# Reordering the first loads of a hybrid decoder layer: norm weights, the second column half of x, and who makes the first operand parts

## The chip, the cores and the metric

The kernel runs on one core of a Trainium2 chip. The metric is the device time of one execution in microseconds (us); less is better. The core has TensorE (PE in the profile, PEld for its weight loads), VectorE (DVE), ScalarE (ACT), GpSimd (POOL) and SyncE (SP), and 16 DMA engines, to which transfers are issued from the queues of SyncE (SP) and ScalarE (ACT) here.

## The reference

One layer, 512 tokens of width 1024, in float32: a SwiGLU block, a token mixer, and a second SwiGLU block, each between two RMS norms, with a residual sum. Only the first block's beginning matters here.

```python
def rms_norm(x, g):
    xf = x.astype(jnp.float32)
    y = xf * lax.rsqrt(jnp.mean(xf * xf, axis=-1, keepdims=True) + RMS_EPS)
    return (y * g.astype(jnp.float32)).astype(x.dtype)

def swiglu(x, w_gu, w_down):
    gate, up = jnp.split(x @ w_gu, 2, axis=-1)
    return (jax.nn.silu(gate) * up) @ w_down

def reference(x, ...):
    for l in range(DEPTH):
        x = x + 0.5 * rms_norm(swiglu(rms_norm(x, ffn1_pre_g[l]), ffn1_w_gu[l], ffn1_w_down[l]), ffn1_post_g[l])
        y = hybrid_mixer(rms_norm(x, mix_pre_g[l]), ...)
        x = x + rms_norm(y, mix_post_g[l])
        x = x + 0.5 * rms_norm(swiglu(rms_norm(x, ffn2_pre_g[l]), ffn2_w_gu[l], ffn2_w_down[l]), ffn2_post_g[l])
    return x
```

`ffn1_w_gu` is 1024 x 5632: its columns 0 to 2815 are the gate weights and those from F = 2816 on the up weights.

## The kernel before

**Products in parts.** A float32 product is made from rounded parts. A value v is split into a high part (v rounded to the matmul's type fp32r) and a low part (v minus the high part). A product of w and x is then three matmuls: high w by high x, low w by high x, high w by low x. For weights the high part is a cast on ScalarE (`first_hi`, L1252) and the low part a subtraction on VectorE or another engine (`first_lo`, L1256). For x the two parts are made from the transposed tile in PSUM, with the norm's weight g1 multiplied in: `turned_high` (L641 on ScalarE, L1233 on VectorE) and `turned_low` (L644 on VectorE). The norm's 1/rms is a factor for each token and comes in after the products.

**Tiles.** x lies in HBM by tokens: 512 tokens are four row blocks (b = 0 to 3) of 128, and each is loaded in two column halves (hf = 0, 1) of 512 columns, so `xn[b][hf]` is 128 x 512, 256 KB. TensorE transposes 128 x 128 squares of it, so that columns of x (c = 0 to 7, 128 each, the sum's index) come to lie on partitions. Columns c = 0 to 3 come from hf = 0 and c = 4 to 7 from hf = 1. Tokens are handled in two halves h of 256: h = 0 needs the row blocks 0 and 1, h = 1 the blocks 2 and 3. One PSUM bank `tps[c]` takes the transposes of two columns c and c + 1 for one h.

**The first weights.** The first 128 gate columns and the first 128 up columns are not loaded by the planner of the later weights, but by `load_first(o, i, *queues)`: o = 0 is gate, o = F is up, and i is which half of the 1024 rows (k = 0 to 3, `lower`; k = 4 to 7, `upper`). One such piece is 128 x 512 in SBUF, 256 KB, in rows of 512 bytes in HBM; where two queues are given, each takes half of it. In the code below, `piece(j, i)`, `first_hi(j, i)` and `first_lo(j, i)` have j = 0 for gate and j = 1 for up.

**The order of the head.** Each engine runs its instructions in the order in which the code writes them. Loads (L449 to L461), by queue: SyncE has x(0,0), half of the gate piece 0, the norm weights g1 (8 rows of 128, 4 KB), x(0,1), x(1,1), the gate piece 1, the up-piece 1, then x(2,0), x(3,0), x(2,1), x(3,1) and the planner's first loads. ScalarE has x(1,0), the other half of the gate piece 0, and the whole up-piece 0. TensorE (L1279 on) has seven warm matmuls on a tile of ones (`spin`, each two records in the profile), the eight transposes of h = 0, c = 0 to 3 (`turn_early`, L1214) with the transpose of g1 (L1216) between the second and the third pair, two more warm matmuls, and then the products of the gate piece 0 with c = 0 to 3 (`passes`, L1289): high by high, low by high. Then come the eight transposes of c = 4 to 7 (`turn`, L1224), which need x(0,1) and x(1,1), then the products with the low parts of x; then the up-piece 0 in three passes, then the pieces 1 (`upper`) of both; then the transposes of h = 1 and the same products for it; and from then on the first matmuls of the next weights, `second`.

**Around it.** ScalarE casts gate piece 0, makes the high parts of c = 0 to 3, casts up-piece 0 and gate piece 1, makes the high parts of c = 4 and 5, and casts up-piece 1. VectorE copies g1 out of PSUM (L1282), subtracts for gate piece 0, makes the low parts of c = 0 to 3, subtracts for up-piece 0 and gate piece 1, makes the high parts of c = 6 and 7, and the low parts of c = 4 to 7. GpSimd subtracts for up-piece 1. From about 22 us on the kernel is one long row of matmuls, whose weights a planner (`Weights`) loads, casts and splits some units ahead.

The load part of the head, with its order:

```python
    load_x(0, 0)
    load_x(1, 0, act)
    load_first(0, 0, act, sync)
    load_first(F, 0, act)
    sync.dma_start(g1rows, rows_of("ffn1_pre_g"))
    for b in range(2):
        load_x(b, 1)
    for o in (0, F):
        load_first(o, 1, sync)
```

Of the kernel before, what the change touches and what calls it, by code (L numbers as in the profile page):

```python
# [20 lines left out]
F = 2816  # L21
# [101 lines left out]
def tile_layer(ctx: ExitStack, tc: tile.TileContext, out: bass.AP, **ins: bass.AP):  # L123
    nc = tc.nc
    pe, dve, act, pool, sync = nc.tensor, nc.vector, nc.scalar, nc.gpsimd, nc.sync
# [16 lines left out]
    def bank(name):  # L142
        return psum.tile([P, T], F32, tag="bank", name=name)

    def t2k(name, dt=F32):
        return big.tile([P, T], dt, tag="t2k", name=name, bufs=NT2K)
# [283 lines left out]
    def rows_of(name):  # L430
        a = ins[name]
        return a[0].rearrange("w (c p) -> (w c) p", p=P) if name == "conv_w" else a[0].rearrange("(c p) -> c p", p=P)
# [3 lines left out]
    g1rows = rows_t[:KD, P:2 * P]  # L436
    first_raw = {}

    def load_x(b, hf, queue=sync):
        queue.dma_start(xn[b][hf], ins["x"][0, b * P:(b + 1) * P, hf * T:(hf + 1) * T])  # L440

    def load_first(o, i, *queues):
        r = first_raw[o, i] = t2k(f"first{o}{i}").rearrange("p (k c) -> p k c", k=4)
        n = 4 // len(queues)
        for j, queue in enumerate(queues):
            r0 = i * T + j * n * P
            queue.dma_start(r[:, j * n:(j + 1) * n], w1[0, r0:r0 + n * P, o:o + P].rearrange("(k p) c -> p k c", p=P))

    load_x(0, 0)  # L449
    load_x(1, 0, act)  # L450
    load_first(0, 0, act, sync)
    load_first(F, 0, act)
    sync.dma_start(g1rows, rows_of("ffn1_pre_g"))
    for b in range(2):
        load_x(b, 1)
    for o in (0, F):
        load_first(o, 1, sync)
    for hf in range(2):
# [67 lines left out]
    def product(w, xs, sl=ALL, name="", hooks=()):  # L526
        ps = bank(name)
        hooks = dict(hooks)
        for k, x in enumerate(xs):
            if k in hooks:  # L530
                hooks[k]()
            mm3(ps[:, sl], w, k, [t[:, sl] for t in x], k == 0, k == len(xs) - 1)
        return ps
# [106 lines left out]
    def x_high(x, src, gain, sl):  # L640
        act.activation(x[0][:, sl], src, AF.Copy, scale=gain)  # L641
# [566 lines left out]
    def turn_early():  # L1208

        tp = [bank(f"xtp{c}0") for c in (0, 2)]  # L1210
        for cc in range(4):
            for i in range(2):
                j = cc % 2
                pe.transpose(tp[cc // 2][:, (2 * j + i) * P:(2 * j + i + 1) * P], xn[i][0][:, cc * P:(cc + 1) * P], ident)  # L1214
            if cc == 1:
                pe.transpose(g1_ps[:, :KD], g1rows, ident[:KD, :KD])  # L1216
        return dict(zip((0, 2), tp))

    def turn(h, c):
        tp = bank(f"xtp{c}{h}")  # L1220
        for j in range(2):
            for i in range(2):
                cc = c + j
                pe.transpose(tp[:, (2 * j + i) * P:(2 * j + i + 1) * P], xn[2 * h + i][cc // 4][:, (cc % 4) * P:(cc % 4 + 1) * P], ident)  # L1224
        return tp

    def turned_high(h, c, tp, eng=act):
        for j in range(2):
            x, g = n1.xs[c + j], g1[:, c + j:c + j + 1]
            if eng is act:  # L1230
                x_high(x, tp[:, HALF[j]], g, HALF[h])
            else:
                dve.tensor_scalar(x[0][:, HALF[h]], tp[:, HALF[j]], g, None, op0=ALU.mult)  # L1233
# [12 lines left out]
    def piece(j, i):  # L1246
        (hi, lo), sl = ws[j], slice(4 * i, 4 * i + 4)
        return hi[:, sl, :], lo[:, sl, :], first_raw[(0, F)[j], i]

    def first_hi(j, i):  # L1250
        hi, lo, raw = piece(j, i)
        act.copy(hi, raw)  # L1252

    def first_lo(j, i, eng=dve):
        hi, lo, raw = piece(j, i)
        eng.tensor_sub(lo, raw, hi.bitcast(F32))  # L1256
# [18 lines left out]
    def spin(n):  # L1275
        for i in range(n):
            pe.matmul(warm[:, (i % 4) * P:(i % 4 + 1) * P], ones.bitcast(F32), ones.bitcast(F32), start=True, stop=True)

    spin(WARM)  # L1279
    g1_ps = bank("g1_ps")  # L1280
    tps = turn_early()
    dve.tensor_copy(g1, g1_ps[:, :KD])  # L1282
    spin(2)
    banks = [bank(f"a_first{i}") for i in range(4)]

    def passes(js, ks, part=0, xpart=0, stop=False, sl=HALF[0]):
# [11 lines left out]

    preload(AF.Copy)
    first_hi(0, 0)  # L1300
    turned_high(0, 0, tps[0])
    turned_high(0, 2, tps[2])
    first_lo(0, 0)
    turned_low(0, 0, tps[0])
# [6 lines left out]
    first_hi(1, 0)  # L1311
    first_hi(0, 1)
    turned_high(0, 4, tps[4])
    first_lo(1, 0)
    first_lo(0, 1)
    turned_high(0, 6, tps[6], dve)
    first_hi(1, 1)
# [11 lines left out]
    tps = {c: turn(1, c) for c in range(0, KD, 2)}  # L1329
# [171 lines left out]
    for g, (f0, f1) in enumerate(GROUPS1):  # L1501
# [20 lines left out]
        for c in range(KD):  # L1522
# [18 lines left out]
            b = pair_banks[c] if c < 2 else product(W.take(), xs, name=f"ya{g}{c}")  # L1541
# [6 lines left out]
    def in_product(name, hooks=(), ahead=AHEAD):  # L1548
        return product(W.take(ahead), mx.xs, name=name, hooks=hooks)
# [81 lines left out]
    for j in range(4):  # L1631
        b = in_product(f"pq{j}")
# [254 lines left out]
    tps = [bank(f"atp{ci}") for ci in range(KC)]  # L1887
# [290 lines left out]
```

## Time and profile before

| what | value |
|---|---|
| device time, median of 3 runs | 835.63 us (835.62 to 835.71) |
| the profiled execution, its own time | 836.39 us |
| its span from first to last instruction | 834.6 us |
| matmul records in the span | 4190 |
| bytes moved by DMA | 144.22 MB, 173 GB/s in the mean |

The page gives the busy time of each engine and its share of the span, then groups of instructions. A row of the timeline is: start in us, length in us, engine, line, operation, written tile and read tiles, shape, count, and in brackets the engine's idle time before it with what ended that. Rows that follow one another are merged, so that a length with x4 covers four. The same row with SPq or ACTq shows the issue of a transfer, not the transfer. A row of the waits is: waiting engine and tile, what it waited for, us in total, times, longest. A row of the windows is: the stretch, its length, for PE, PEld, DVE, ACT and POOL the busy time and (count), then TensorE's granted clock, the busy share of the DMA engines, and GB/s.

### The profile page before, as it was taken

To read this page: it belongs to the slowest core of one execution; us is meant where nothing else is said; L and a number is where in the kernel's file an instruction comes from. 1 tells how busy PE (TensorE), PEld (TensorE's weight loads), DVE (VectorE), ACT (ScalarE), POOL (GpSimd) and SP (SyncE) were. 2 spreads that over 40 slices of the span, in tenths; PEclk is the share of its full clock that TensorE was granted. 3 is DMA by queue.
4 is the path that set the end of the run, shared out by engine and by line. 5 is a ranking of instruction groups with operands and counts; after the bars stand their busy time and mean duration, and the time that the engine had idled before them with its cause. 6 is when DMAs were issued, how large, how long until landed. Compare 5 with 4: busy or idle time off the path is not lost.

```text
span 834.6 us, 11761 instructions
## 1 busy us (share of the span) xinstructions
PE 826.2 (99%) x4190; PEld 701.0 (84%) x4190; DVE 733.8 (88%) x1031; ACT 520.0 (62%) x813; POOL 165.5 (20%) x187
## 2 busy tenths in 40 slices
PE   9999999999999999999999999999999999999996
PEld 8888888888888898987788899888888888888885
DVE  5989799998989978888789689998999798898996
ACT  6756756676666654556897446545757677676562
POOL 1022000140320325414531052002005023032001
PEclk9999999999999999999999999999999999999999
DMA  7376408398595797523511140567339949669742
GB/s 254 103 252 244 159 12 308 89 266 259 127 260 180 186 281 230 188 78 94 164 45 51 51 138 15 124 179 253 128 107 240 308 96 250 233 161 261 298 139 102
DMA packets 121835, 144.22 MB, mean 173 GB/s; under 512 B 24168, under 2 KB 76720, under 8 KB 121264
## 3 DMA queue, kind: packets, MB, share of 16 engines
q1 hardware_dynamic: 106896, 112.26, 42.0%
q0 software_dynamic: 13792, 30.42, 16.6%
q10 hardware_dynamic: 1088, 0.79, 0.3%
q8 instruction: 33, 0.54, 0.3%
q14 instruction: 26, 0.21, 0.1%
HBM read 100.45 MB, written 39.32 MB: 167 GB/s over the span
## 4 chain that ended last, share of the span: by engine, by line
PE 98%; DMA 1%; DVE 0%; SPq 0%; issue 0%; DVEq 0%
PE ab L1026 10%; PE aa L1026 10%; PE db L1026 5%; PE da L1026 5%; PE yaa L1427 3%; PE bb L1026 3%; PE ya L1427 3%; PE ba L1026 3%; PE a_first L1289 3%; PE yda L1427 2%; PE aa L956 1%; PE yab L2016 1%; PE yab L2017 1%; PE yab L2018 1%; PE wo L1942 1%; PE gt L522 1%
## 5 line engine op out<-in xcount | busy, mean ns | idle before, releaser
L1198 POOL DMA_DIRECT2D yr_a<-stage x36 | 31.2, 1015 | 175.7 <-ACT stage L1195 153.8
L1198 POOL DMA_DIRECT2D yp_b<-stage x42 | 36.5, 1070 | 146.3 <-ACT stage L1195 120.0
L2032 POOL DMA_DIRECT2D yp_b<-stage x8 | 4.4, 547 | 64.7 <-ACT stage L2031 64.3
L745 POOL TENSOR_TENSOR acca_r<-acca_r,sq_r 128x512 f32<-128x512 f32 x6 | 9.1, 1509 | 38.2 <-ACT sq_r L552 38.1
L540 PE MATMUL an<-xh_mx,whi_xl 128*128 128x256 f32 x64 | 15.7, 285 | 0.0
L541 PE MATMUL an<-xh_mx,wlo_xl 128*128 128x256 f32 x64 | 15.5, 283 | 0.0
L2136 POOL TENSOR_TENSOR last<-yp,grow 128x512 f32<-128x512 f32 x3 | 3.9, 1291 | 57.0 <-DVE yp L2126 57.0
L2133 ACT ACTIVATE ysq<-yp 128x512 f32<-128x512 f32 (+1 forms) x8 | 4.9, 607 | 15.7 <-DVE yp L2126 15.7
L522 PE MATMUL gt<-xh_mx,whi_gt 128*128 128x512 f32 x32 | 14.2, 443 | 0.0
L1464 POOL DMA_DIRECT2D yp_a<-zy x16 | 8.7, 554 | 25.5 <-DMA rows_a<-yr_a 17.2
L498 ACT ACT_TABLE_LOAD x9 | 11.5, 1283 | 2.4 <-issue 2.3
L522 PE MATMUL pq<-xh_mx,whi_q 128*128 128x512 f32 x32 | 12.8, 400 | 0.0
L524 PE MATMUL gt<-xh_mx,wlo_gt 128*128 128x512 f32 x32 | 12.6, 394 | 0.0
L522 PE MATMUL pgb<-xh_f,whi_bg 128*128 128x512 f32 x32 | 12.6, 393 | 0.0
L523 PE MATMUL gt<-xl_mx,whi_gt 128*128 128x512 f32 x32 | 12.5, 392 | 0.0
L524 PE MATMUL pq<-xh_mx,wlo_q 128*128 128x512 f32 x32 | 12.5, 391 | 0.0
L523 PE MATMUL pq<-xl_mx,whi_q 128*128 128x512 f32 x32 | 12.5, 390 | 0.0
L524 PE MATMUL pgb<-xh_f,wlo_bg 128*128 128x512 f32 x32 | 12.5, 390 | 0.0
L524 PE MATMUL pub<-xh_f,wlo_bu 128*128 128x512 f32 x32 | 12.5, 390 | 0.0
L523 PE MATMUL pub<-xl_f,whi_bu 128*128 128x512 f32 x32 | 12.5, 390 | 0.0
L522 PE MATMUL pub<-xh_f,whi_bu 128*128 128x512 f32 x32 | 12.5, 389 | 0.0
L523 PE MATMUL pgb<-xl_f,whi_bg 128*128 128x512 f32 x32 | 12.5, 389 | 0.0
(2028 smaller groups left out, 3397.8 us busy)
## 6 DMA issues: line engine op xcount, KB each, us to landing
yp_b<-stage POOLq DMA_DIRECT2D x50, 256.0 KB, 9.0
yr_a<-stage POOLq DMA_DIRECT2D x44, 256.0 KB, 9.8
h_a<-za SPq DMA_DIRECT2D x16, 256.0 KB
h_b<-zb SPq DMA_DIRECT2D x16, 256.0 KB
hxb<-h_b SPq DMA_DIRECT2D x16, 256.0 KB
hxa<-h_a SPq DMA_DIRECT2D x6, 512.0 KB
raw_ad<-in_ffn_w_down SPq DMA_DIRECT2D x2, 1024.0 KB
xT_hbm<-xT POOLq DMA_DIRECT2D x2, 1024.0 KB, 6.1
```

Of the source, the lines that this page charges most:

```text
L498: act.activation(dummy, eps, func)
L522: pe.matmul(ps, hi[:, k, :], xh, start=start, stop=False)
L523: pe.matmul(ps, hi[:, k, :], xl, start=False, stop=False)
L524: pe.matmul(ps, lo[:, k, :], xh, start=False, stop=stop)
L540: pe.matmul(ps[:, sl], hi[:, k, :], xh, start=k == 0 and not goes_on, stop=False, skip_group_check=True)
L541: pe.matmul(ps[:, sl], lo[:, k, :], xh, start=False, stop=False, skip_group_check=True)
L745: eng.tensor_add(acc, acc, square(part, ALL, f"{self.name}{c}"))
L1026: pe.matmul(b[tb], x[:, blk], w[:, k, :], start=first and q + k + j == 0, stop=q + k == 2 and j == 2, skip_group_check=True)
L1198: pool.dma_start(o, st, accum_op=ALU.add)
L1289: pe.matmul(banks[j][:, sl], ws[j][part][:, k, :], n1.xs[k][xpart][:, sl], start=k == 0 and part == xpart, stop=stop and k == KD - 1)
L1427: pe.matmul(o, x[:, blk], a[:, k, :], start=start and j == 0, stop=stop and j == 2, skip_group_check=True)
L1464: (pool if q % 2 else sync).dma_start(chunks[32 * q:32 * (q + 1), :, i * P:(i + 1) * P], turned[32 * i:32 * (i + 1), :, q])
```

## The change

The loads of the head are put in another order and partly on another queue. The norm weights go second on SyncE's queue, ahead of half of the gate piece 0. x(0,1) stays on SyncE's queue and x(1,1) goes to ScalarE's, third there; the up-piece 0 leaves ScalarE's queue for SyncE's, behind x(0,1). SyncE's later loads keep their order. TensorE transposes g1 after the first pair of transposes instead of the second, and has one warm matmul less ahead of the products. VectorE instead of ScalarE makes the high parts of c = 0 and 1. GpSimd instead of VectorE subtracts for the up-piece 0.

```diff
     load_x(0, 0)
     load_x(1, 0, act)
+    sync.dma_start(g1rows, rows_of("ffn1_pre_g"))
     load_first(0, 0, act, sync)
-    load_first(F, 0, act)
-    sync.dma_start(g1rows, rows_of("ffn1_pre_g"))
-    for b in range(2):
-        load_x(b, 1)
+    load_x(0, 1)
+    load_x(1, 1, act)
+    load_first(F, 0, sync)
     for o in (0, F):
         load_first(o, 1, sync)
...
                 pe.transpose(tp[cc // 2][:, (2 * j + i) * P:(2 * j + i + 1) * P], xn[i][0][:, cc * P:(cc + 1) * P], ident)
-            if cc == 1:
+            if cc == 0:
                 pe.transpose(g1_ps[:, :KD], g1rows, ident[:KD, :KD])
...
     tps = turn_early()
     dve.tensor_copy(g1, g1_ps[:, :KD])
-    spin(2)
+    spin(1)
     banks = [bank(f"a_first{i}") for i in range(4)]
...
     first_hi(0, 0)
-    turned_high(0, 0, tps[0])
+    turned_high(0, 0, tps[0], dve)
     turned_high(0, 2, tps[2])
...
     turned_high(0, 4, tps[4])
-    first_lo(1, 0)
+    first_lo(1, 0, pool)
     first_lo(0, 1)
```

## The prediction

> **What bounds the kernel now.** First the page: the span and the busy shares.
>
> ```profile
> span 834.6 us, 11761 instructions
> PE 826.2 (99%) x4190; PEld 701.0 (84%) x4190; DVE 733.8 (88%) x1031; ACT 520.0 (62%) x813; POOL 165.5 (20%) x187
> ```
>
> TensorE is idle for 834.6 - 826.2 = 8.4 us in all. Next the waits of TensorE over the whole span, and the part of the chain that ended last that lies in the head.
>
> ```profile
> PE warm L1277 <- DVE eps L488: 1.1, 1, 1.1
> PE xtp L1224 <- DMA xn<-in_x: 0.8, 2, 0.5
> ```
> ```profile
> 2.57 6.90 DMA xn<-in_x
> 9.47 0.04 issue
> 9.52 0.98 PE xtp L1224 x7
> 10.50 4.91 PE a_first L1289 x40
> ```
>
> The reader is to see that TensorE waits only twice before its last work: 1.1 us at the start, and 0.8 us for the second column half of x; the rest of the 8.4 us lies behind its last matmul. From 9.52 on it has no gap that this view counts, so what it gains in the head moves the whole program, and it can gain only there. The timeline of TensorE in the head (start, length, line):
>
> ```profile
> 4.27 1.08 PE L1214 MATMUL xtp<-ident,xn 128*128 128x128 f32 x4
> 5.28 0.27 PE L1216 MATMUL g_ps<-ident,rows 8*128 8x8 f32 x1
> 5.49 1.11 PE L1214 MATMUL xtp<-ident,xn 128*128 128x128 f32 x4
> 6.39 0.86 PE L1277 MATMUL warm<-ones 128*128 128x128 f32 x4
> 7.00 0.91 PE L1289 MATMUL a_first<-xh_a,whi_first 128*128 128x256 f32 x4
> 7.75 0.64 PE L1289 MATMUL a_first<-xh_a,wlo_first 128*128 128x256 f32 x4
> 9.52 0.98 PE L1224 MATMUL xtp<-ident,xn 128*128 128x128 f32 x7 [0.55 <-DMA xn<-in_x]
> 10.26 0.72 PE L1289 MATMUL a_first<-xl_a,whi_first 128*128 128x256 f32 x4
> 10.81 0.64 PE L1289 MATMUL a_first<-xh_a,whi_first 128*128 128x256 f32 x4
> 12.25 1.21 PE L1289 MATMUL a_first<-xh_a,whi_first 128*128 128x256 f32 x8
> 15.24 1.91 PE L1224 MATMUL xtp<-ident,xn 128*128 128x128 f32 x16
> ```
>
> **TensorE's own path, change by change.** Matmuls overlap, so pace is start to start. Four transposes in 1.08 us, the last taking 0.42, are 0.22 apiece; the seven at 9.52 take 0.74 to the next group. The two gains before the wait for x come from these engines' rows:
>
> ```profile
> 5.14 0.62 ACT L1252 CAST whi_first<-first 128x512 fp32r<-128x512 f32 x1 [1.36 <-DMA first<-in_ffn_w_gu]
> 5.79 1.69 ACT L641 ACTIVATE xh_a<-xtp,g 128x256 fp32r<-128x256 f32 x4
> 9.70 1.33 ACT L1252 CAST whi_first<-first 128x512 fp32r<-128x512 f32 x2 [2.22 <-DMA first<-in_ffn_w_gu]
> ```
> ```profile
> 5.59 0.17 DVE L1282 COPY g<-g_ps 128x8 f32<-128x8 f32 x1 [4.49 <-PE g_ps L1216]
> 5.79 0.69 DVE L1256 TENSOR_TENSOR wlo_first<-first,whi_first 128x512 fp32r<-128x512 f32 x1
> 6.66 1.72 DVE L644 SCALAR_TENSOR_TENSOR xl_a<-xtp,g,xh_a 128x256 fp32r<-128x256 f32 x4 [0.18 <-ACT xh_a L641]
> 11.67 0.87 DVE L1233 TENSOR_SCALAR xh_a<-xtp,g 128x256 fp32r<-128x256 f32 x2
> ```
>
> The gains g1 are 4 KB. Second on SyncE's queue they follow only the first x piece, which the transposes at 4.27 already had, so I take them as there at 4.7; their transpose moves one pair ahead. Today it starts at 5.28, where the pace (4.27 + 5 x 0.22 less rounding) would allow 5.14. That returns 0.15, and without the restart up to 0.2: the second four end their issue near 6.2. One warm matmul less is two of the four records at 6.39, at 0.22 each: 0.4 off. The products with xh_0 start near 6.6 instead of 7.00. Both cuts lie wholly on the path, as TensorE has no wait there; if g1 landed as late as now, the 0.2 would be back.
>
> VectorE now makes xh_0 and xh_1: g1 copied from about 5.0 to 5.2, then two at 0.44 (the pair at L1233 took 0.87) to 6.1. Then its subtraction, 0.69, to 6.75 and four xl at 0.42 to 8.4, as late as now (6.66 + 1.72 = 8.38). ScalarE has only xh_2 and xh_3 left, done near 6.9 instead of 7.48. So the four products with whi go from 6.6 to about 7.2 (the first two at 0.22, then 0.12, as the row at 10.81 has it), the four with wlo (wlo ready 6.75) to 7.7. Eight transposes at 0.11 follow to 8.55, **if x is there**, and the xl products start at 8.55 to 8.7 instead of 10.26; xl_3 at 8.4 is in time. That is the ceiling: **1.6 us, at most 1.7**, and nothing behind it can add more, since there is no later wait in the list to remove.
>
> **Is the data there?** The queue's own waits, SyncE's issues, and the DMA traffic by stretch (last column GB/s):
>
> ```profile
> SPq L440 <- DMA first<-in_ffn_w_gu: 3.4, 1, 3.4
> ...
> SPq L447 <- DMA xn<-in_x: 1.1, 1, 1.1
> ```
> ```profile
> 4.15 0.93 SPq L447 DMA_DIRECT2D first<-in_ffn_w_gu  x2
> 5.12 5.38 SPq L440 DMA_DIRECT2D xn<-in_x  x4
> ```
> ```profile
> 0.00:4.00 4.00, 2.88 (x13) 2.88 (x14) 0.20 (x5) 1.49 (x2) 0.70 (x6) 1.00 0.49 158
> 4.00:6.00 2.00, 2.00 (x11) 1.59 (x10) 0.38 (x2) 0.83 (x2) 0.00 (x0) 1.00 0.76 214
> 6.00:8.00 2.00, 2.00 (x14) 1.87 (x13) 1.82 (x5) 1.47 (x4) 0.00 (x0) 1.00 0.92 288
> 8.00:10.00 2.00, 1.20 (x9) 0.81 (x8) 0.39 (x1) 0.30 (x1) 0.00 (x0) 1.00 1.11 370
> ```
>
> Moved by 4, 6, 8 and 10 us: 0.63, 1.06, 1.64, 2.38 MB. A piece (half a row block of x, or one piece of weights) is 0.262 MB. Today the whole up-piece goes third on ScalarE's queue, beside both second halves of x, which go fourth and fifth on SyncE's. With it moved behind x(0,1), five pieces and g1, 1.32 MB, are to be moved when x(1,1) is complete; 1.58 when the up-piece is; 1.84 when the next gate piece is. I read three bounds off the rows.
>
> - At 0.33 MB/us from 4.0 on (mean of the two last rows; the 4 to 6 stretch has its engines idle a quarter of the time, and I take that dip to be the many small rows of the up-piece) and 0.5 us from last byte to use (at that rate back from 4.0, the 0.52 MB of the first two x pieces had moved by 3.7; the issue at 4.15 had waited for the first of them, by the 1.1 us row): x at 6.6, up-piece 7.4, gate piece 8.2.
> - At today's rates with 0.5: 7.4, 8.3, 9.1.
> - At today's rates with today's lag of 1.8 (1.58 MB by 7.8, but transposes at 9.52; 1.84 by 8.55, second cast near 9.70 + 1.33 - 0.62 = 10.41): 8.7, 9.6, 10.4.
>
> I take the first, as the change takes out what the dip is made of; nearest to it is the 8 to 10 row. x is then there a microsecond before TensorE asks (7.7).
>
> **The next limit** is the pair of weight pieces. ScalarE casts the up-piece 0.65 after it lands: F + 0.65 = 8.05, where TensorE wants it at 9.2 (8.65 and the 0.55 from 10.26 to 10.81). GpSimd subtracts it now:
>
> ```profile
> 12.36 1.30 POOL L1256 TENSOR_TENSOR wlo_first<-first,whi_first 128x512 fp32r<-128x512 f32 x1 [10.98 <-ACT whi_first L1252]
> 20.14 2.42 POOL L215 TENSOR_TENSOR wlo_second<-raw_second,whi_second 128x1024 fp32r<-128x1024 f32 x1 [6.49 <-DMA rows<-in_b_rg]
> ```
> ```profile
> 20.68 2.96 DVE L215 TENSOR_TENSOR wlo_second<-raw_second,whi_second 128x1024 fp32r<-128x1024 f32 x1
> 28.43 1.22 DVE L215 TENSOR_TENSOR wlo_ag<-raw_ag__107,whi_ag 128x1024 fp32r<-128x1024 f32 x1
> ```
>
> 1.30 instead of 0.69 on VectorE, to F + 1.98 = 9.4, wanted two groups of 0.48 after that, at 10.2 (three of them lie between 10.81 and 12.25): hidden. But the same VectorE subtraction takes 1.22 alone and 2.96 beside GpSimd's. Of the 2.96, 1.88 lay inside GpSimd's 2.42, and 1.08 behind it, nearly the whole job: VectorE stood still. So the gate piece's subtraction may end only 0.62 after GpSimd's, at F + 2.6 = 10.0; two xh at 0.87 and xh_7 is there at F + 3.47 = 10.9. Today xh_7 ends at 11.67 + 0.87 = 12.54 and TensorE, at 12.25 and 0.12 apiece, needs it at 12.6; shifted by 1.6 that is 11.0. Just in time. The Trainium skill, SBUF — State Buffer, section "SBUF: two separate sides", states that pair of ports as an exclusive lock that blocks the loser for a whole instruction; the rows above agree. By that rule the sum stays 1.6 while F is under 7.5 and loses a microsecond for each one that F is later; without it the later gate piece would rule (G + 2.2 = 10.4).
>
> Other costs at nothing: SyncE's 3.4 us wait, in the middle of its last four x issues, ends when the up-piece lands, near 9.7. Counting the loads in order, each from the ninth on waits for the one eight before; that partner is now the first gate piece, so the issue comes near 6. That helps x(2,1) and x(3,1), whose transposes start at 15.24 with no wait; cover 0. ScalarE's third issue is as long as the one it replaces. Behind 12.25 every product follows at pace. The later loads hold up ScalarE once:
>
> ```profile
> ACT whi_au L210 <- DMA raw_au__380<-in_ffn_w_gu: 1.8, 1, 1.8
> ```
>
> TensorE waits for nothing there. If those loads came no sooner, some of the gain could be lost; bound 0 to 0.3, I take 0.
>
> **Sum.** 0.2 (g1) + 0.4 (warm) + 0.2 (xh earlier) + 0.8 (x there) = 1.6; a tenth off for an edge at xh_7: **-1.5 us**. In the profiled execution 836.39 (span 834.6, 1.8 around it) becomes 834.9. The three timed runs have a median of 835.63, 0.76 lower, with the same work; the forecast is 835.63 - 1.5 = **834.1**.
>
> **The rivals.**
> 1. The loads come at today's rates (7.4, 8.3, 9.1) and GpSimd holds VectorE: xh_7 at F + 3.47 = 11.8, so 12.54 - 11.8 = 0.75 gained, 834.9; without the hold 1.2. For it: the 2.96 row. Against: the dip.
> 2. The change doesn't do what it says: x's halves land no sooner, as the same engines move the same bytes. The Trainium skill, Trainium Kernel Development and Optimization, "Key Constraints", speaks for this: queues share 16 engines, and several issuers save issue time alone. Worked from rows: only the up-piece's 0.26 MB go from ahead of x, 0.8 us at 0.33 MB/us: x at 8.7, xl products at 9.6, at best 0.65 gained; with late weights 0 to 0.6, about 835.3.
> 3. **Slower: the up-piece, now behind x, lands too late, and GpSimd's subtraction holds VectorE.** With the third bound F = 9.6, xh_7 at 13.05 against 12.54: +0.5, 836.1. It decides from F over 9.05. For it: today's 1.8 us lag. Against: the lag grew up beside the up-piece's own traffic.
> 4. The clock. The granted clock in the rows above is 1.00 throughout, yet the pace goes from 0.22 to 0.11 inside the warm group at 6.39 (four records in 0.86). The Trainium skill, TensorE: Matmul & The Clock Gate, "Part 1: The HAM clock gate", says the full rate comes after a busy window of about 3.4 us, free-running; with less warm work a gap could cost a window. From rows: at 0.22 until 10.3, the products end at 8.3, transposes at 10.05, and xl starts at 10.05 to 10.26: the gain is gone, 835.6. Against: the stretch to 6.9 has no gap more than now, rather 0.15 less.
>
> **How the numbers follow.** Forecast 0.58 (gain 1.2 to 1.7); rival 1, 0.19; rival 2, 0.10; rival 3, 0.09; rival 4, 0.04. The range holds forecast, rival 1 and part of 2: 833.85 to 835.2. A measurement can tell about 0.2%, 1.67 us. The ceiling lies right at that: of the forecast I give a fifth to over 1.67, so faster 0.12; slower by over 0.2% needs the clock lost for two windows, 0.02; within 0.2%, 0.86.
>
> **What would show it.** Right: no DMA wait before the second transposes, xl products near 8.6, the group now at 12.25 near 10.7, GpSimd's subtraction near 8. Rival 1: a gap of TensorE before xh_7 while VectorE's subtraction is longer than 0.69. Rivals 2 and 3: waits for xn or for whi_first from the up-piece. Rival 4: a pace of 0.22 after 7. Wrong altogether: a wait behind 20 us that is not in the list now.

## The result

| kernel | median, us | lowest to highest | runs |
|---|---|---|---|
| before | 835.76 | 835.33 to 836.54 | 20 |
| after | 837.11 | 835.95 to 839.82 | 20 |

The ratio is 1.0017, with a 95% interval of 1.0010 to 1.0024. The change makes the kernel 1.35 us slower where 1.5 us less was forecast, and the time is outside the range of 833.85 to 835.2. The times of after also spread over 3.9 us, those of before over 1.2. The profiled execution of after took 837.06 us, 0.05 under its median; that of before, 836.39, lay 0.63 above its own. So the two profiles show only some 0.7 of the 1.35. Of the runs below, one of e1 took 1009.0 us at a granted clock of 0.77 and one of the kernel before 914.0 us at 0.85, in a slower state, and both are left out everywhere.

### The profile page after: what moved, and what is told of

Same layout as the page of the kernel before. It is cut to its first block, busy times and chain, and to the rows that moved or that the text cites. A ratio compares the mean times of both kernels' runs of the same rounds, so it can differ in the third digit from the quotient of the medians.

```text
span 835.2 us, 11759 instructions
## 1 busy us (share of the span) xinstructions
PE 826.8 (99%) x4188; PEld 701.0 (84%) x4188; DVE 735.1 (88%) x1032; ACT 519.1 (62%) x811; POOL 165.5 (20%) x188
## 4 chain that ended last, share of the span: by engine, by line
PE 94%; DVE 3%; DMA 1%; ACT 1%; issue 1%; POOL 0%; SPq 0%; DVEq 0%; POOLq 0%; ACTq 0%
PE ab L1026 10%; PE aa L1026 10%; PE db L1026 5%; PE da L1026 5%; PE yaa L1427 3%; PE a_first L1289 3%; PE bb L1026 3%; PE ba L1026 3%; PE ya L1427 3%; PE yda L1427 2%; PE aa L956 1%; PE yab L2016 1%; PE yab L2018 1%; PE yab L2017 1%; PE wo L1942 1%; DVE xc L1572 1%
```

## The profile after

Page of after: span, busy time of each engine, and one queue.

```profile
span 835.2 us, 11759 instructions
PE 826.8 (99%) x4188; PEld 701.0 (84%) x4188; DVE 735.1 (88%) x1032; ACT 519.1 (62%) x811; POOL 165.5 (20%) x188
...
q8 instruction: 33, 0.54, 0.3%
```

The last row, one of the DMA queues (packets, MB, share), is needed further down. All waits of TensorE in after, to be read beside the two of before:

```profile
PE warm L1277 <- DVE eps L488: 1.1, 1, 1.1
PE a_first L1289 <- ACT whi_first L1252: 0.4, 1, 0.4
PE cur L1724 <- DVE home L1613: 0.3, 1, 0.3
```

The wait for x is gone, as forecast. Two came in its place: one for the first gate weights, and one at L1724, in the token mixer at 404 us. The prediction had named a wait behind 20 us as the sign that it is wrong altogether.

**The head gained 0.6 to 0.7 us.** Timeline of TensorE in after:

```profile
4.89 0.27 PE L1216 MATMUL g_ps<-ident,rows 8*128 8x8 f32 x1
...
7.44 1.12 PE L1289 MATMUL a_first<-xh_a,whi_first 128*128 128x256 f32 x4 [0.44 <-ACT whi_first L1252]
8.40 0.64 PE L1289 MATMUL a_first<-xh_a,wlo_first 128*128 128x256 f32 x4
8.88 1.04 PE L1224 MATMUL xtp<-ident,xn 128*128 128x128 f32 x8
9.67 0.72 PE L1289 MATMUL a_first<-xl_a,whi_first 128*128 128x256 f32 x4
11.67 1.12 PE L1289 MATMUL a_first<-xh_a,whi_first 128*128 128x256 f32 x8
14.55 1.69 PE L1224 MATMUL xtp<-ident,xn 128*128 128x128 f32 x14
```

The group with xl starts at 9.67 (before 10.26), the first products of the upper pieces at 11.67 (12.25), the transposes of h = 1 at 14.55 (15.24). The second transposes follow at 8.88 without a gap, so x is there. What holds the head back is its beginning: the first product is at 7.44, where 6.6 was forecast and before had 7.00. ScalarE, VectorE and GpSimd of after say why and what else came true:

```profile
6.77 0.62 ACT L1252 CAST whi_first<-first 128x512 fp32r<-128x512 f32 x1 [3.02 <-DMA first<-in_ffn_w_gu]
...
8.24 1.38 ACT L1252 CAST whi_first<-first 128x512 fp32r<-128x512 f32 x2
```
```profile
9.65 1.13 DVE L1256 TENSOR_TENSOR wlo_first<-first,whi_first 128x512 fp32r<-128x512 f32 x1
10.71 0.86 DVE L1233 TENSOR_SCALAR xh_a<-xtp,g 128x256 fp32r<-128x256 f32 x2
```
```profile
8.95 1.29 POOL L1256 TENSOR_TENSOR wlo_first<-first,whi_first 128x512 fp32r<-128x512 f32 x1 [7.57 <-ACT whi_first L1252]
```

The cast of the first gate piece starts at 6.77 after a wait for its load; before it started at 5.14. Half of that piece is SyncE's, and now stands behind g1 there. GpSimd's subtraction holds VectorE's as forecast, 1.13 instead of 0.69, and xh_7 is ready at 10.71 + 0.86 = 11.57, for a group that starts at 11.67: no wait.

**The mixer lost 1.2 us.** SyncE's issues around 395 us, before and then after:

```profile
395.22 0.46 SPq L1583 DMA_DIRECT2D ig<-r  x1
395.80 0.53 SPq L1585 DMA_DIRECT2D ig<-other  x1
```
```profile
394.57 0.46 SPq L1583 DMA_DIRECT2D ig<-r  x1
395.14 1.41 SPq L1585 DMA_DIRECT2D ig<-other  x1
```

After runs 0.65 earlier here, but its second issue takes 0.88 longer. Next GpSimd, which waits for that transfer, and VectorE, before and then after:

```profile
398.26 1.80 POOL L1587 TENSOR_TENSOR xc<-ig,xc 128x512 f32<-128x512 f32 x1 [1.50 <-DMA ig<-other]
402.53 2.17 POOL L1587 TENSOR_TENSOR xc<-ig,xc 128x512 f32<-128x512 f32 x1 [0.66 <-DMA ig<-other]
```
```profile
402.35 1.21 DVE L215 TENSOR_TENSOR wlo_gt<-raw_gt__3749,whi_gt 128x1024 fp32r<-128x1024 f32 x1
403.48 0.28 DVE L1613 TENSOR_TENSOR home<-pq,R_mx 128x128 f32<-128x128 f32 x1
```
```profile
398.47 1.29 POOL L1587 TENSOR_TENSOR xc<-ig,xc 128x512 f32<-128x512 f32 x1 [2.38 <-DMA ig<-other]
401.51 1.76 POOL L1587 TENSOR_TENSOR xc<-ig,xc 128x512 f32<-128x512 f32 x1
```
```profile
402.05 2.30 DVE L215 TENSOR_TENSOR wlo_gt<-raw_gt__3748,whi_gt 128x1024 fp32r<-128x1024 f32 x1
404.28 0.28 DVE L1613 TENSOR_TENSOR home<-pq,R_mx 128x128 f32<-128x128 f32 x1
```

The reader is to see who starts first. Before, VectorE's subtraction starts at 402.35 and GpSimd's `xc` at 402.53: VectorE takes its 1.21, GpSimd is stretched to 2.17, and TensorE has no wait. After, the first `xc` waits 2.38 instead of 1.50, VectorE's chain behind it slips, the second `xc` starts at 401.51 and VectorE at 402.05: now VectorE is stretched, to 2.30, `home` comes at 404.28 instead of 403.48, and TensorE waits for it. The order turns by both: against a program that is 0.65 earlier, VectorE starts 0.35 later and the second `xc` 0.37 earlier, as it no longer waits for its transfer (0.66 before). Why that transfer is there sooner isn't shown. A little later TensorE's transposes `pt` slip as well, before and then after:

```profile
408.63 0.60 PE L1779 MATMUL pt<-ident,sc 128*128 128x128 f32 x4
```
```profile
408.63 1.10 PE L1779 MATMUL pt<-ident,sc 128*128 128x128 f32 x4
```

From 0.7 ahead in the head, after is level at 408.63 and takes 0.50 longer for these four; that makes 1.2, and at the end of the span after is 0.6 behind.

What differs at 395 us is one packet. DMA traffic of after in the two microseconds from the first of these issues on, by queue (packets, MB, share):

```profile
q1 hardware_dynamic: 77, 0.13, 27.9%
q8 instruction: 1, 0.02, 3.7%
q0 software_dynamic: 5, 0.00, 0.8%
```

The same stretch of before, 395.22 to 397.22, has no packet of q8. By the row of the page, a packet of q8 is 0.54 MB / 33, 16 KB. The Trainium skill, Runtime: NRT & Kernel Launch, section "Instruction fetch mechanics", says that an engine's instructions are fetched in blocks of 16 KiB, 256 instructions. 2 x 4188 records of TensorE make 32.7 such blocks, so q8 fits TensorE's stream. The change takes four records out of that stream, one warm matmul: from there on each block should be called for four instructions later. That is **theory F**: the shorter stream puts a fetch into these issues and turns the order of GpSimd and VectorE round. Its rival in the first four runs is that the stream's length doesn't matter and the loss belongs to the new order of the head as a whole.

## The experiments

Each kernel was timed in 11 runs (e1 in 10), beside the kernel before on the same chip. m3 and m4, further down, are two more profiles of e1's kernel, with one time each. The ratio is estimated from all runs and isn't the quotient of the two medians.

| run | median, us (lowest to highest) | before, same chip | ratio, 95% interval |
|---|---|---|---|
| e1: change, both warm matmuls | 836.53 (835.29 to 838.38) | 835.91 | 1.0009, 1.0000 to 1.0018 |
| e2: before, one warm matmul less | 837.13 (836.34 to 838.19) | 835.91 | 1.0018, 1.0008 to 1.0027 |
| e3: e1, g1 behind the gate half | 835.64 (835.24 to 837.28) | 835.91 | 0.9999, 0.9990 to 1.0008 |
| e5: change, a matmul added later | 836.65 (835.19 to 838.54) | 835.91 | 1.0013, 1.0004 to 1.0022 |
| n1: e2, a matmul added later | 835.98 (835.80 to 836.16) | 835.84 | 1.0003, 0.9994 to 1.0011 |
| n2: e3, one warm matmul less | 837.01 (835.59 to 837.65) | 835.84 | 1.0009, 1.0000 to 1.0018 |
| n3: before, a matmul added later | 835.99 (835.56 to 836.70) | 835.84 | 1.0003, 0.9994 to 1.0011 |
| n4: the order of the loads alone | 835.16 (834.98 to 835.68) | 835.84 | 0.9993, 0.9985 to 1.0002 |
| m1: change, three warm matmuls | 835.99 (835.49 to 837.40) | 836.12 | 1.0000, 0.9991 to 1.0009 |
| m2: n4, a warm matmul moved later | 835.45 (835.07 to 835.90) | 836.12 | 0.9993, 0.9984 to 1.0002 |

### One warm matmul (e1, e2, n1, n3)

e1 is the changed kernel with the warm matmul back. e2 is the kernel before without it.

```diff
-    spin(1)
+    spin(2)
```

> The changed kernel with its second warm matmul back (two in place of one), nothing else. Theory F (instruction fetch): with one warm matmul less, TensorE's stream is four instructions shorter, so the 16 KB block that its queue fetches near 395 us is fetched later against the program and meets the small transfer ig<-r of the mixer. With the four instructions back the mixer keeps the timing of the kernel before, no wait of TensorE for home near 404, and the head keeps its 0.7 us, as the second warm matmul ends before the wait for the first weight cast is over: 835.76 - 0.7 = 835.1, 834.8 to 835.5. Rival P (phase): the mixer is late because everything ahead of it came 0.7 us sooner or because SyncE's queue held 384 packets more: then the loss stays, 837.1 (836.7 to 837.5).

```diff
-    spin(2)
+    spin(1)
```

> The kernel before with one warm matmul in place of two, nothing else. Theory F: the head does not change, as TensorE waits for x at 9.5 anyway, but the fetch moves as in the changed kernel: the mixer loses 0.6 to 2 us, 836.4 to 837.8, and the runs scatter more than those of before (1.2 us from least to most). Rival P: 835.8, within 0.3.

e2 has nothing of the change but a missing warm matmul, and 837.13 is what the whole change takes. By the rival, P, e2 should have come out at 835.8. Its head is as fast as before's, so the loss is not there. The issue in question and two of TensorE's waits in e2:

```profile
395.70 1.22 SPq L1585 DMA_DIRECT2D ig<-other  x1
```
```profile
PE xtp L1224 <- DMA xn<-in_x: 0.9, 2, 0.5
...
PE cur L1724 <- DVE home L1613: 0.2, 1, 0.2
```

The long issue and the wait at `cur` are both there. The profiled execution of e2 took 836.68, so it shows less than the whole loss. e1, at 836.53 (836.76 in the expectations, which count the run of 1009.0 us), fits neither theory: the matmul is back, and about half of the loss stays. So there is a second cause, taken up below.

n1 puts the four instructions back, but some 27 us later, where they can do nothing for the head:

```diff
-    spin(2)
+    spin(1)
...
         pe.transpose(cols_ps[:, :n_rows], rows, ident[:n_rows, :n_rows])
+        pe.matmul(cols_ps[:, P:2 * P], ones.bitcast(F32), ones.bitcast(F32), start=True, stop=True)
```

> The kernel before with one warm matmul less (spin(1)), and one matmul of the same kind put into make_cols some 25 us later, so that all instructions of TensorE behind make_cols stand again where they stood in the kernel before. Theory F (the place of the 16 KB instruction fetches in TensorE's stream sets the loss near 395 us): it comes out like the kernel before, 835.6 to 836.1, and TensorE does not wait at cur. Theory C (the work missing in the head costs, wherever the instructions stand): like the run with one warm matmul less, 836.9 to 837.4.

n1 took 835.98, and its slowest run is faster than the fastest of e2. Its profile has the short issue again, and no wait at `cur`:

```profile
395.56 0.53 SPq L1586 DMA_DIRECT2D ig<-other  x1
```

So it isn't the work missing in the head that costs e2 its 1.2 us, but the place of all later instructions in TensorE's stream. n3 has the added matmul alone, four instructions more than before:

> The kernel before with one more matmul in make_cols, four instructions of TensorE more and nothing else moved; about 0.3 us of added work. Theory F in its wide form (any shift of the fetches by four instructions can cost): anything from 835.6 to 837.2, slower than before by over 0.5 if the kernel before stands at a favourable place. Theory C: 835.9 to 836.3, the added work alone. It says how much a shift of the stream by itself is worth where the head is untouched.

835.99, no more than the added work: four instructions more are harmless, four fewer aren't.

### g1 ahead of the gate half (e3, n2, e5)

e3 is e1 with one line moved; it differs from the change in that line and in the warm matmul.

```diff
-    sync.dma_start(g1rows, rows_of("ffn1_pre_g"))
     load_first(0, 0, act, sync)
+    sync.dma_start(g1rows, rows_of("ffn1_pre_g"))
```

> As e1_warm_back, and the norm weights behind SyncE's half of the first gate piece instead of ahead of it. In the changed kernel that half landed only for the cast at 6.77, against 5.14 before. Theory H1 (the small load ahead of it delays the half): the cast comes at 5.2 to 5.8, TensorE's first product near 7.0 instead of 7.44, and the head gains a further 0.3 to 0.7 us: with theory F 834.3 to 834.8. Theory H2 (x(1,1) on ScalarE's queue or the up-piece behind it delays the half): the cast stays at 6.5 to 7.0 and the time at that of e1_warm_back, within 0.3.

835.64 against e1's 836.53, and the spread is gone but for one run. The first cast starts at 5.28 again. Beside the one at the start, TensorE has these waits in e3:

```profile
PE g_ps L1216 <- DMA rows<-in_ffn_pre_g: 0.2, 1, 0.2
PE a_first L1289 <- POOL wlo_first L1256: 0.2, 1, 0.2
```

So the wait of 0.2 for g1, which the change was to remove, is cheaper than the late weights. The order of the issues explains only a part of these: SyncE issues the half at 1.66 in after and at 1.25 in e3, 0.4 apart, while the casts are 1.5 apart; where the rest comes from isn't shown. In the last row GpSimd's slower subtraction for the up-piece, hidden in after, reaches TensorE.

n2 is e3 with `spin(1)`: the good order of loads, and the short stream.

> The changed kernel with the small load of the norm weights moved behind SyncE's half of the first gate piece, with one warm matmul less as in the changed kernel. Against the run with both warm matmuls and the same order of loads (835.64). Theory F: the four missing instructions bring the collision back, 836.4 to 837.0 with a wait at cur of some 0.2 to 0.3. Theory C (a gap in TensorE's work in the head costs, and this order of loads has none of the first gate piece): 835.4 to 835.8 and no such wait.

837.01: the 1.2 of e2 come back, 1.4 here. Five of the 11 runs lie between 835.59 and 836.19 and six between 837.01 and 837.65, so the median says little here (by the means n2 is 0.9 above e3). That fits a collision in some executions only, but none of the five was profiled. The profile of n2, a time at 837, has the long issue and the largest wait at `cur` of all:

```profile
394.66 1.58 SPq L1585 DMA_DIRECT2D ig<-other  x1
```
```profile
PE cur L1724 <- DVE home L1613: 0.7, 1, 0.7
```

Over the profiles the sign is without exception (m3 and m4 stand for e1's kernel). After, e2 and n2, the three with one warm matmul less and nothing in its place, show a q8 packet in the 2 us from the issue of `ig<-r` on and an issue of 1.22 to 1.58; the nine others and before have no such packet, and 0.52 to 0.65. In these ten the packet starts 0.4 to 0.9 ahead of the issue of `ig<-r`, in the three 0.4 to 0.5 behind it. The order of the engines goes with it: counted from that issue, VectorE's subtraction starts at 7.1 and the second `xc` at 7.3 in all ten, but `xc` at 6.9 to 7.1 and VectorE at 7.3 to 8.9 in the three. One thing theory F doesn't explain: in n3 and m1, with four instructions more than before, the packet isn't earlier than in before.

e5 is the changed kernel with the matmul of n1 added, so with its own head and the stream's length of before.

> The changed kernel, with one matmul of the same form as the warm one put beside the transpose of the parameter columns near 34 us, into a part of that bank that nothing reads: TensorE's stream has its length back from there on, while the head is as in the changed kernel. It costs 0.2 us of TensorE. Theory F: the mixer is as before, 835.76 - 0.7 + 0.2 = 835.3 (835.0 to 835.7). Rival W (the second warm matmul matters in the head itself): 837.3. Rival P: 837.3.

Its profile has the short issue and no wait at `cur`, but the times run from 835.19 to 838.54, as those of e1 do. So e5, at 836.65, is no better than e1: theory F's mechanism held, its forecast of 835.0 to 835.7 didn't. What e1, e5 and after share, and e3 and n4 lack, is g1 ahead of the gate half.

### Why the times spread (m1, m3, m4)

m1 is the changed kernel with `spin(3)`; m3 and m4 are one profile each of e1's kernel.

> The changed kernel with three warm matmul pairs behind the first transposes (spin(3)) in place of one, so that TensorE has work until its first weights are there at 7.1 to 7.8 us, and its stream has four instructions more than in the kernel before. What is open is why the change with both warm matmuls back still has a median of 836.76 and single times up to 838.4. Theory C (a gap of TensorE ahead of its first product lets the clock come to full speed a window of 3.4 us later in some executions): without the gap the times draw together, 835.6 to 836.4 and none above 837. Theory L (SyncE's half of the first gate piece, behind the norm weights, lands at a time that differs from execution to execution): the late half is as late as before, so the times stay spread, a median of 836.5 to 837.0 with some above 837.5. Theory F expects no wait at cur in it.

> The changed kernel with both warm matmuls again, one profile, since that of its timed runs was a disturbed one. Theory F: no wait at cur and the issue of ig<-other takes some 0.53 us again, whatever the time of this execution. Theory L: the first cast of the gate piece starts between 6.0 and 7.1 us, and a late one goes with a long time: about 835.5 with 6.0 to 6.4, 836 to 836.5 with 6.7 to 7.1. Theory C: a time above 837 shows the products of the head at half speed for some 3 us longer.

> The same kernel as in the run ahead of it, a second profile: same expectations. Two looks are too few for the spread of the times, but they say whether the start of the first cast, or the speed of the head's products, goes with the time of the execution.

m3 and m4 ran the same kernel and took 835.40 and 837.38 us. TensorE's first products, second transposes and first products with xl, m3 and then m4:

```profile
6.88 1.12 PE L1289 MATMUL a_first<-xh_a,whi_first 128*128 128x256 f32 x4 [0.36 <-ACT whi_first L1252]
8.32 1.04 PE L1224 MATMUL xtp<-ident,xn 128*128 128x128 f32 x8
9.11 0.72 PE L1289 MATMUL a_first<-xl_a,whi_first 128*128 128x256 f32 x4
```
```profile
7.87 1.32 PE L1289 MATMUL a_first<-xh_a,whi_first 128*128 128x256 f32 x4 [1.65 <-ACT whi_first L1252]
9.84 1.78 PE L1224 MATMUL xtp<-ident,xn 128*128 128x128 f32 x8
11.38 0.72 PE L1289 MATMUL a_first<-xl_a,whi_first 128*128 128x256 f32 x4
```

In m4 the weights are 1.0 later, and then the same eight transposes take 1.78 instead of 1.04. The windows of m4 (the number ahead of the last two columns is the granted clock):

```profile
4.50:7.90 3.40, 1.75 (x14) 1.37 (x13) 1.09 (x4) 0.70 (x2) 0.00 (x0) 1.00 0.99 294
7.90:11.35 3.45, 3.45 (x16) 3.38 (x17) 3.07 (x6) 2.19 (x6) 1.28 (x1) 0.51 1.07 372
11.35:14.80 3.45, 3.45 (x30) 3.45 (x29) 2.44 (x6) 3.26 (x11) 1.30 (x1) 1.00 1.12 349
```

TensorE is busy for 1.75 of 3.40 us, and in the 3.45 after that its clock is 0.51; then it is whole again. m3 has 1.00 in each of these windows, with 3.04 busy in the first. 11.38 - 9.11 = 2.3 us is the difference at the products with xl, and 2.0 that of the whole execution: of the 2.3, 1.0 lies ahead of the first product (7.87 - 6.88), with the late weights, and 1.3 behind it, with the low clock. The Trainium skill, TensorE: Matmul & The Clock Gate, "Part 1: The HAM clock gate", gives windows of 3413 ns that run free, and a fall to half rate after at least one idle window. The length agrees; the fall came here after a window half busy.

Both theories behind these expectations have a share, then: L (the half's landing varies) opens the gap, and C (the clock) doubles its price in m4, the one profile with a long gap. Gaps of 0.4 to 0.8 in m3, after, m1 and e5 left the clock at 1.00. That the gap makes the clock fall rests on this one profile and was not tested by an edit. The start of the first cast in the profiles shows the variation: 4.93 to 5.58 in e3, n2, n4 and m2, but 6.77, 7.09, 6.70, 6.21 and 7.20 in after, e5, m1, m3 and m4. How the spread divides between L and C was not measured further. m1 didn't settle it: its median of 835.99 is 0.5 under e1's, as C has it, yet three pairs of warm matmuls left a gap of 0.6 in its profile, and one run took 837.4.

### The order of the loads alone (n4, m2)

```diff
     load_first(0, 0, act, sync)
-    load_first(F, 0, act)
     sync.dma_start(g1rows, rows_of("ffn1_pre_g"))
-    for b in range(2):
-        load_x(b, 1)
+    load_x(0, 1)
+    load_x(1, 1, act)
+    load_first(F, 0, sync)
```

> The kernel before with the order of the loads alone: x's second halves ahead of the up-weights' piece on both queues, the norm weights behind SyncE's half of the first gate piece. Both warm matmuls, the transpose of the norm weights, the engines of the first x parts and of the low parts are those of before. If the order of the loads carries the whole gain of the head: as with all of the change but the two parts undone, 835.5 to 835.8 (a head 0.6 to 0.9 shorter). If the engines carry a part: 835.8 to 836.1. Theory F expects no wait at cur in it, since TensorE's stream has all its instructions.

835.16, 0.68 under before's 835.84; each of its 11 runs is below that median. The interval of the ratio reaches 1.0002, though. TensorE in n4:

```profile
8.41 1.03 PE L1224 MATMUL xtp<-ident,xn 128*128 128x128 f32 x8
9.20 0.72 PE L1289 MATMUL a_first<-xl_a,whi_first 128*128 128x256 f32 x4
...
11.19 1.12 PE L1289 MATMUL a_first<-xh_a,whi_first 128*128 128x256 f32 x8
...
14.07 1.91 PE L1224 MATMUL xtp<-ident,xn 128*128 128x128 f32 x16
```

10.26 - 9.20, 12.25 - 11.19 and 15.24 - 14.07: 1.1 to 1.2 gained in the head, with VectorE subtracting for the up-piece as before, and no wait but 0.2 for g1. Its median is the lowest of all versions, though its lead over before is not clear of the noise.

> The order of the loads alone (835.16), with one warm matmul less and one of the same kind added in make_cols, as in the run on the kernel before. If the warm matmul was on the path in the new order too: the head gets 0.2 to 0.4 shorter and make_cols 0.2 longer, 834.9 to 835.2. If the first products then wait for their weights or for x's parts instead: 835.1 to 835.4. Theory C, if the missing warm matmul opens a gap: times spread up to 837.

m2, with one warm matmul moved behind the head, took 835.45, 0.67 under the before of its chip: no more than n4. In its profile the products with xl start at 8.63, but the time doesn't show a further gain; that stays open.

## Why the prediction was wrong

**"What it gains in the head moves the whole program, and it can gain only there"**, and with it the costs behind the head, "bound 0 to 0.3, I take 0": this step failed. It took TensorE's waits of before as the whole account, but work that has no wait can get one. The head's gain did move the program, up to 404 us; there the profile of after loses 1.2, and by the medians the removed warm matmul costs 1.15 to 1.4 (e2 against n1, n2 against e3). The term of 0.4 for "one warm matmul less" counted only its time, not that four instructions of TensorE's stream go. As a time it was too large as well: in the prediction's own rows the four records at 6.39 take 0.61 to the next group, so two are worth 0.3.

**"Second on SyncE's queue they follow only the first x piece"**: the terms of 0.2 for g1 and 0.2 for an earlier xh were mis-sized, to below nothing. g1 was there in time (transposed at 4.89 without a wait), but what it was put ahead of was not counted: half of the first gate piece. Its cast went from 5.14 to 6.77 and the first product to 7.44 instead of 6.6. That is 0.84 of the 1.0 by which the products with xl come later than forecast (9.67 against 8.65). The rest goes in the first four products, 0.96 instead of 0.6 (8.40 - 7.44): ScalarE makes xh_2 and xh_3 only behind the late cast. In other executions it costs more, with the low clock of m4: e1 is 0.89 above e3.

**The data.** x was there at 8.88 without a wait. For the landing of the up-piece, F, the bound taken, 7.4, was too early. In after its cast starts at 8.24, behind ScalarE's other work; in e3 and n2 ScalarE waits for the piece until 8.41 and 8.09. That is near the second bound, 8.3. xh_7 at 11.57 agrees with F + 3.47 for an F of 8.1. That VectorE's subtraction ends some 0.6 behind GpSimd's was forecast rightly: 9.65 + 1.13 = 10.78 against 8.95 + 1.29 = 10.24.

The late F is a second term of the head that was mis-sized. n2 shows it, as g1 is behind the gate half there and the products with xl start at 8.60, as forecast. Its group of the upper pieces, and VectorE's last two high parts:

```profile
10.73 1.62 PE L1289 MATMUL a_first<-xh_a,whi_first 128*128 128x256 f32 x8
```
```profile
10.57 0.86 DVE L1233 TENSOR_SCALAR xh_a<-xtp,g 128x256 fp32r<-128x256 f32 x2
```

The group starts near the 10.7 of the forecast, but xh_7 is ready only at 11.43, and the group takes 1.62 instead of the 1.12 of after. The transposes of h = 1 come at 14.10, 1.1 earlier than before's 15.24, where 1.5 was forecast.

**The rivals.** Rival 3 had the right sign by a mechanism that didn't occur: the up-piece came by 8.1 to 8.4, ahead of the 9.05 that this rival needs. Rival 4, the clock, was dismissed as there would be "no gap more than now"; that rested on the first cast at 5.14, so it fell with the term for g1. m4 shows it. No rival had the fetch.

**The sum.** The steps from n4 to after, one edit at a time: 835.16 for the loads with g1 behind; +0.48 with the engines and the place of g1's transpose as in the change (e3); +0.89 with g1 ahead (e1); +0.58 with one warm matmul less (after, 837.11). These are differences of medians from several sets of runs, in which the kernel before differs by up to 0.36, so the 0.48 and the 0.58 are not clear of it; and they depend on the order: taken out of e3, the warm matmul costs 1.37 (n2), and g1 ahead then adds only 0.10. Undone in the change by itself, either part gives back 0.6 or less (e1, e5, n2); undone together they give back 1.47 (e3).

What is not taken apart is whether the fetch itself lengthens the issue. The two went together in every profile, and the four instructions decide over both; a fetch moved without them was not tried.

## What to carry over

A list of an engine's waits says where it can gain, not where it can lose: before an edit is costed at nothing, look for the places where two engines start within some tenths of a microsecond of each other on work that excludes the other, since a shift turns their order round. Here a load of 4 KB put ahead of one of 128 KB made the large one late, so price what stands behind a moved load, not only what is ahead. And where one median is odd, look at the spread: two profiles of the same kernel, of executions 2 us apart, told more than many medians.

## What was not expected of the hardware

- Taking four instructions out of TensorE's stream at 6 us cost the kernel before 1.15 us (e2 against n1), lost near 404 us, and putting four in at 34 us brought it back.
- An issue on SyncE's queue of 0.53 us took 1.22 to 1.58 where a 16 KB instruction packet fell in the same 2 us. The Trainium skill, Runtime: NRT & Kernel Launch, "Instruction fetch mechanics", has the cost of crossing a block as mostly hidden. For TensorE's own work it is hidden here, as no row shows TensorE waiting for one; whether it holds these transfers is not shown, only that the two go together.
- A load of 8 rows, 4 KB, ahead of half a weight piece delayed the cast of that piece by 0.6 to 2.3 us (6.21 to 7.20 against 4.93 to 5.58).
- A single gap of 1.65 us in TensorE's work was followed by 3.4 us at a clock of 0.51, in one profile (m4).
